# Transposed projection pieces on normed x, in matmuls of 512 columns

## The chip, the cores and the metric

One core of a Trainium2 chip runs one hybrid decoder layer. The metric is the device time of one execution in microseconds, the median of several runs. The engines are TensorE (PE, with its weight loads PEld), VectorE (DVE), ScalarE (ACT), GpSimd (POOL) and SyncE (SP, which here only issues DMAs). Each engine executes its own list of instructions in the order in which the program issues them, and an instruction that waits holds back those behind it on its engine.

## The reference, cut to what matters

The input x has 256 tokens by 1024 channels. The layer normalizes x, multiplies it by one large projection matrix, feeds the columns to four token mixers and a set of gates, merges the branches, and adds an FFN.

```
def rmsnorm(x, w):
    y = xf * lax.rsqrt(jnp.mean(xf * xf, axis=-1, keepdims=True) + NORM_EPS)
    return y * w

h = rmsnorm(x, norm_mix[l])
proj = h @ w_in
(m_z, m_xbc, m_dt, b_qkv, c_qkv, c_f, d_q, d_kv, gate_logits) = jnp.split(proj, SPLIT_POINTS, axis=-1)
y_a = mamba2_branch(m_z, m_xbc, m_dt, ...)     # conv over tokens, SiLU, scan
y_b = moba_attention(bq, bk, bv, ...)
y_c = forgetting_attention(cq, ck, cv, c_f + forget_bias)
y_d = sliding_window_attention(dq, dk, dv, sinks, ...)
gates = sigmoid(gate_logits)
x = x + sum(gates * branch_out) @ w_out
x = x + swiglu(rmsnorm(x, norm_ffn[l]), ...)
```

The factor rsqrt(...) belongs to a token, so it may be multiplied in before the projection or after it.

## The kernel before

**Products in two parts.** Each float32 matrix is split into a hi part (rounded by ACT, `split_hi`) and a lo part (the rest, by DVE, `split_lo`). A product is hi times hi, hi times lo, and lo times hi. The weights come in pieces, named in `FIRST`: `xbc0 n0 qkB0 vB0 vB1 xbc2 qkB1 xbc3 z0 ...`, then gates (`g...`), branch and output projections, `gu` and `dn` of the FFN. A piece is fetched (`fetch`, SP), split in two chunks and multiplied. Three buffers each hold raw, hi and lo weights.

**x of the projection.** `xx(k)` holds channels 128k to 128k+127 of x times `norm_mix`, transposed, as a hi and a lo half of 256 tokens each, side by side. The token factor is not in it. It is multiplied in when a product leaves PSUM: `rb` holds it as a row (times 1, 0.125 and 0.5), `r1` and `r1h` as a column.

**Transposed pieces.** For pieces `qk`, `xbc`, `z` and `qD` the weights (128 columns at a time) are the stationary operand, and the result has channels on partitions. `tr_groups` does two groups for a piece, one for each 128 columns; both fill halves of one PSUM bank. A group is built by `two` and `mm`: for each of 8 k, hi weights times the hi half of x (L264), the same hi weights times the lo half (L265), and after these 8 times lo weights times the hi half (L262): 24 matmuls of 256 columns, each with a weight load of its own. One DVE instruction then takes both halves out of PSUM times `rb`: `end_scaled` (L936) for qk and qD, the first lines of `conv` (L630) and `silu_z` (L661). In natural pieces (`v`, `g`, L1044) x is the stationary operand and weights stream in 512 columns.

**FFN.** Pieces `gu4` and up already work in the other manner: `wide` (L273, L277) multiplies hi weights by both halves of the normalized `x3x` in one matmul of 512 columns, then lo weights by the hi half in 256 columns; `end_ffn` adds the halves of the bank by an ACT copy (L1180) and a DVE addition (L1181).

**The planner.** `Weaver` decides while the program is written where the other engines' work is placed. It holds a clock in nanoseconds for PE, DVE and ACT. `wv.tick(GROUP)` after a group adds 2620 to the PE clock, steps the urgent tasks once, issues chunks of the split (68 + 1.043n on the DVE clock: 1136 for a chunk of 1024) and then steps the other tasks in the order of their list. A task is a generator; each `yield Need(...)` gives the cost of its next step and the buffers that it needs. A step of a task that isn't urgent is refused if it would bring the DVE or ACT clock over the PE clock plus `SLACK` (3500), if the task is ready more than 60 after the clock, or if it has matmuls and is ready over 300 after the PE clock. `wv.until(flags)` asks for none of this: in passes over the list it runs one step of each task for which buffers are free, until the flags are set.

**The tasks at the start.** `conv(0)`, `conv(1)` and `softplus_cums` are started after the first group of qkB0. `softplus_cums` has a DVE reciprocal, then some 27 small POOL instructions (L548 to L564) that end in `av`, then matmuls on `av` (`cum_n`), a DVE copy to `cumn` (L571), two transposes (`cum_t`) and a store. `bias_rows` makes bias rows in `es` and stores them to DRAM. `cb_products` (L674, L675) follows `conv(0)` and `conv(1)`. PSUM has 3 banks tagged acc and 5 tagged att.

Of the kernel before, what the change touches and what calls it, by code (L numbers as in the profile page):

```python
# [25 lines left out]


FIRST = ("xbc0 n0 qkB0 vB0 vB1 xbc2 qkB1 xbc3 z0 qkB2 z1 qkB3 qD0 qkC0 vC0 vC1 qkC1 qD1 qkC2 qkC3").split()

# [177 lines left out]
def hybrid_block_kernel(ctx: ExitStack, tc: tile.TileContext, A, out):  # L207
# [270 lines left out]
        return flat(p)  # L478


    def nat_groups(name, hi, lo, n=256):

        if n == 256:
            p = acc(name, [128, 2, 256])
        else:
            p = [att("%s_%d" % (name, t), [128, n]) for t in range(2)]
        hb, lb = cut(hi, 8, n), cut(lo, 8, n)
        for t in range(2):
            group(p[:, t, :] if n == 256 else p[t],
                  three((lambda k: hb[:, k, :], lambda k: lb[:, k, :]), at_tok(xx, t), range(8)))  # L490
            yield p
# [19 lines left out]
    def bias_rows():  # L511

        yield Need(pe=680, att=1)
        p = att("e", [128, 384])
        for i in range(2):
            pe.matmul(p[32 * i : 32 * i + 8, :], tab[:, 8 * i : 8 * i + 8], oneh[:, i, :], start=True, stop=True)
        yield Need(act=840, w2=2)
        for i in range(2):
            es = work("es%d" % i, [8, 384], "w2")
            act.activation(es, p[32 * i : 32 * i + 8, :], AF.Copy)  # L520
            nc.sync.dma_start(erow[8 * i : 8 * i + 8, :], es)
        rel(att=1, w2=2)
        wv.done.add("erow")

    def softplus_cums():

# [96 lines left out]

    def conv(i, p):

        yield Need(dve=650, w2=2)
        u = work("cu%d" % i, [128, 2, 259], "w2")
        dve.memset(u[:, :, 0:3], 0.0)
        if i > 1:
            dve.tensor_tensor(u[:, :, 3:259], p, rb2(1), ALU.mult)  # L630
            rel(acc=1)
        else:
            for j in range(2):
                dve.tensor_tensor(u[:, j, 3:259], p[j], rb[:, 1, :], ALU.mult)
            rel(**{("att", "acc")[i]: 2})
        c = work("cc%d" % i, [128, 2, 256], "w2")
        th = u[:, :, 0:256]
        for k in range(4):
            if k < 2:
                yield Need(act=620) if k == 0 else Need(dve=800)  # L640
            elif k == 2:
                yield Need(dve=1600)
            for j in range(2):
                g = (2 * i + j + 4) % 8
                if k == 0:
                    act.activation(c[:, j, :], u[:, j, 0:256], AF.Identity, scale=tapsh[:, g, 0:1],
                                   bias=tapsh[:, g, 4:5])
                else:
                    dve.scalar_tensor_tensor(c[:, j, :], u[:, j, k : k + 256], tapsh[:, g, k : k + 1], c[:, j, :],
                                             ALU.mult, ALU.add)  # L650
        act.activation(th, c, AF.Tanh)
        wv.act += 520
        yield Need(dve=1200)
        half_silu(bc[i] if i < 2 else xs[:, 2 * i - 4 : 2 * i - 2, :], c, th)
        rel(w2=2)
        wv.done.add("xbc%d" % i)

    def silu_z(i, p):
        yield Need(dve=600, act=520, w2=2)
        zh = work("zh%d" % i, [128, 2, 256], "w2")  # L660
        dve.tensor_tensor(zh, p, rb2(2), ALU.mult)  # L661
        rel(acc=1)
        th = work("zt%d" % i, [128, 2, 256], "w2")
        act.activation(th, zh, AF.Tanh)
        yield Need(dve=600)
        half_silu(zs[:, 2 * i : 2 * i + 2, :], zh, th)
        rel(w2=2)
        wv.done.add("z%d" % i)

    def cb_products():  # L670
        for g in range(2):
            yield Need(pe=650, att=1)
            p = att("cb%d" % g, [128, 384])
            pe.matmul(p[:, 0:256], bc[0][:, g, 0:128], bc[1][:, g, :], start=True, stop=True)  # L674
# [256 lines left out]
        wv.later(lambda js=js: fox_quad(js), ["qkC%d" % j for j in js] + ["vC0", "vC1", "cum"], True)  # L931


    def end_scaled(name, o, p, r):
        yield Need(dve=600)
        dve.tensor_tensor(o, p, r, ALU.mult)  # L936
        rel(acc=1)
        wv.done.add(name)

    def end_v(br, t, p):  # L940
        yield Need(act=620)
        if br not in v:
            v[br] = slot("v" + br, (128, 2, 512))
        act.activation(v[br][:, t, :], p, AF.Copy, scale=r1[:, t : t + 1])
        rel(acc=1)
        wv.done.add("v%s%d" % (br, t))

    def end_of(name, p):
# [5 lines left out]
        if name[:2] == "qk":  # L954
            br = name[2]
            if i % 2 == 0:
                qk[br, i // 2] = slot(name)
            return end_scaled(name, qk[br, i // 2][:, 2 * (i % 2) : 2 * (i % 2) + 2, :], p, rb[:, 0:2, :])
        if name[:2] == "qD":
            if i == 0:  # L960
                qD.append(slot("qD"))
            return end_scaled(name, qD[0][:, 2 * i : 2 * i + 2, :], p, rb2(0))

    def end_gate(b, nh, t, p):
        yield Need(act=570)
        if nh == 0:
            gates[b, t] = slot("gate%d%d" % (b, t), (128, 1024))
        act.activation(gates[b, t][:, 512 * nh : 512 * nh + 512], p, AF.Tanh, scale=r1h[:, t : t + 1])  # L968
        rel(acc=1)


# [41 lines left out]
            rel(att=1)  # L1013
        wv.done.add("mt%d" % nh)

    rb = const("rb", [128, 3, 256])
    pg = {}
    r1n, r1h = const("r1n", [128, 2]), const("r1h", [128, 2])
    for name in names[1 : names.index("wo00")]:
        if name[:2] == "wb":  # L1020
            b, nh = int(name[2]), int(name[3])
            br = "ABCD"[b]
# [11 lines left out]
        if name[0] in "gv":  # L1034
            b, nh, kh = (int(c) for c in name[1:]) if name[0] == "g" else (name[1], 0, int(name[2]))
            hi, lo = take(name)
            hb, lb = cut(hi, 4, 512), cut(lo, 4, 512)
            for t in (1, 0) if kh else (0, 1):
                if kh == 0:
                    pg[t] = acc("p%s%d" % (name[:-1], t))  # L1040
                terms = three((lambda k: hb[:, k, :], lambda k: lb[:, k, :]),
                              lambda k: xx(4 * kh + k)[:, :, tok(t)], range(4))
# [7 lines left out]
        hi, lo = take(name)  # L1050
        n = sizes[name] // 8
        for p in (nat_groups(name, hi, lo, n) if name[0] == "n" else
                  tr_groups(name, hi, lo, n)):
# [2 lines left out]
        if name == "n0":  # L1056
# [7 lines left out]
            dve.tensor_scalar(r1h, r1, 0.5, None, ALU.mult)  # L1064
# [4 lines left out]
            for i, f in enumerate((1.0, 0.125, 0.5)):  # L1069
                act.activation(rb[:, (1, 0, 2)[i], :], prow, AF.Copy, scale=f)  # L1070
            rel(att=1)
        if name != "n0":
            wv.add(end_of(name, p))
# [305 lines left out]
```

## Time and profile before

| | |
|---|---|
| median of 3 runs | 511.09 us (510.99 to 511.87) |
| the profiled execution, its own time | 511.23 us |
| span, first to last instruction | 509.5 us |
| busy: PE, DVE, ACT, POOL | 501.6, 352.5, 285.6, 30.6 us |
| stretch of the pieces qkB1 to qkC3 | about 48 to 143 us |

The profiled execution's own time lies 1.73 us over its span. Busy time of an engine is the sum of its instructions; the chain of waits is the path from the last instruction back through what released each. In the chain each matmul stands with the time by which it moves the end (its distance from its neighbour), in the timeline with its whole duration, a longer one since matmuls overlap.

### The profile page before, as it was taken

Reading aid. Unit: us, or ns where it says so; the run is one execution under the profiler, and the core shown is the slowest. Engines: PE = TensorE matmul, PEld = TensorE weight load, DVE = VectorE, ACT = ScalarE, POOL = GpSimd, SP = SyncE. Lnnn points to the kernel's source line nnn. Section 1 sums busy time; section 2 is a strip of 40 time slices with the busy share of each in tenths; the row PEclk is TensorE's granted clock in tenths of the full one; section 3 lists DMA queues with packets and bytes.
Section 4 is the critical chain, followed back from the end, with each engine's and each line's share of the span. In section 5 each row is a group of like instructions: output and inputs, shape, how many; then the busy total and the mean of one; then the engine's idle time right before and its main releaser. Section 6 shows DMA issues by size and latency. Waiting matters only on the chain.

```text
span 509.5 us, 7926 instructions
## 1 busy us (share of the span) xinstructions
PE 501.6 (98%) x3106; PEld 443.7 (87%) x3106; DVE 352.5 (69%) x655; ACT 285.6 (56%) x507; POOL 30.6 (6%) x58
## 2 busy tenths in 40 slices
PE   8999999999999999999999999999999999999995
PEld 8988999979988878788888899998888888888884
DVE  5697589697874969496393675688767766764524
ACT  6687356557565747645534435776566655734322
POOL 0008110011220100000000000000000000000000
PEclk9999999999999999999999999999999999999998
DMA  8965545555555464336267291546455445675202
GB/s 307 388 246 185 198 154 214 203 182 180 173 189 184 131 236 152 125 132 282 82 227 268 100 334 67 188 150 237 164 180 219 180 170 204 248 259 222 98 0 82
DMA packets 16161, 96.06 MB, mean 189 GB/s; under 512 B 1979, under 2 KB 2651, under 8 KB 5884
## 3 DMA queue, kind: packets, MB, share of 16 engines
q1 hardware_dynamic: 14844, 91.36, 49.1%
q0 software_dynamic: 1280, 4.20, 2.9%
q8 instruction: 24, 0.39, 0.3%
q14 instruction: 13, 0.11, 0.1%
HBM read 94.46 MB, written 1.09 MB: 188 GB/s over the span
## 4 chain that ended last, share of the span: by engine, by line
PE 96%; DMA 1%; issue 1%; DVE 0%; SPq 0%; ACT 0%; POOLq 0%; POOL 0%
PE pg L1044 17%; PE gu L273 13%; PE pd L1238 11%; PE pb L262 9%; PE gu L277 7%; PE pvC L1044 2%; PE pvB L1044 2%; PE xbc L451 2%; PE qkC L264 2%; PE qkB L262 2%; PE po L262 2%; PE gu L262 2%; PE qkC L265 2%; PE qkC L262 2%; PE qkB L264 2%; PE gu L265 2%
## 5 line engine op out<-in xcount | busy, mean ns | idle before, releaser
L273 PE MATMUL gu<-x3x,hi_gu 128*128 128x512 f32 x288 | 68.7, 391 | 0.0
L1044 PE MATMUL pg<-hi_g,xx 128*128 128x512 f32 x256 | 64.3, 393 | 0.0
L273 PEld LDWEIGHTS gu<-x3x,hi_gu 128*128 128x128 f32 x288 | 52.9, 188 | 10.2
L355 DVE TENSOR_TENSOR lo_gu<-raw_gu,hi_gu 128x1024 fp32r<-128x1024 f32 x44 | 53.3, 1222 | 6.2 <-ACT hi_gu L347 6.2
L1044 PEld LDWEIGHTS pg<-hi_g,xx 128*128 128x128 f32 x256 | 47.4, 188 | 11.0 <-issue 1.5
L1238 PE MATMUL pd<-hi_dn,aa 128*128 128x512 f32 (+1 forms) x176 | 46.6, 387 | 0.0
L347 ACT ACTIVATE hi_g<-raw_g 128x1024 fp32r<-128x1024 f32 x32 | 32.9, 1053 | 23.6 <-DMA raw_g<-in_w_dram 15.7
L347 ACT ACTIVATE hi_gu<-raw_gu 128x1024 fp32r<-128x1024 f32 x44 | 44.0, 1048 | 1.6 <-PE gu L265 1.6
L355 DVE TENSOR_TENSOR lo_dn<-raw_dn,hi_dn 128x1024 fp32r<-128x1024 f32 x22 | 26.1, 1222 | 21.9 <-ACT hi_dn L347 21.8
L355 DVE TENSOR_TENSOR lo_g<-raw_g,hi_g 128x1024 fp32r<-128x1024 f32 x32 | 38.7, 1236 | 2.7 <-ACT hi_g L347 2.7
L1238 PEld LDWEIGHTS pd<-hi_dn,aa 128*128 128x128 f32 x176 | 32.9, 188 | 6.6
L277 PEld LDWEIGHTS gu<-x3x,lo_gu 128*128 128x128 f32 x288 | 36.9, 191 | 1.4
L277 PE MATMUL gu<-x3x,lo_gu 128*128 128x256 f32 x288 | 37.4, 283 | 0.0
L347 ACT ACTIVATE hi_dn<-raw_dn 128x1024 fp32r<-128x1024 f32 x22 | 22.2, 1051 | 25.2 <-PE pd L1238 25.2
L1044 PE MATMUL pg<-lo_g,xx 128*128 128x512 f32 x128 | 34.2, 389 | 0.0
L1181 DVE TENSOR_TENSOR gs<-gu,ge 128x256 f32<-128x256 f32 x36 | 15.2, 424 | 20.1 <-ACT ge L1180 20.1
L1044 PEld LDWEIGHTS pg<-lo_g,xx 128*128 128x128 f32 x128 | 24.0, 188 | 5.0
L1180 ACT ACTIVATE ge<-gu 128x256 f32<-128x256 f32 x36 | 13.8, 384 | 25.5 <-PE gu L277 25.5
L1238 PE MATMUL pd<-lo_dn,aa 128*128 128x512 f32 (+1 forms) x88 | 26.9, 387 | 0.0
L355 DVE TENSOR_TENSOR lo_wb<-raw_wb,hi_wb 128x1024 fp32r<-128x1024 f32 x16 | 19.4, 1221 | 7.4 <-ACT hi_wb L347 7.4
L968 ACT ACTIVATE gate<-pg,r1h 128x512 f32<-128x512 f32 x16 | 11.0, 689 | 20.0 <-PE pg L1044 19.9
L347 ACT ACTIVATE hi_wb<-raw_wb 128x1024 fp32r<-128x1024 f32 x16 | 16.7, 1055 | 7.3 <-PE pg L1044 5.5
(323 smaller groups left out, 1115.9 us busy)
## 6 DMA issues: line engine op xcount, KB each, us to landing
raw_gu<-in_w_dram SPq DMA_DIRECT2D x22, 1024.0 KB, 4.8
raw_g<-in_w_dram SPq DMA_DIRECT2D x16, 1024.0 KB, 4.8
raw_dn<-in_w_dram SPq DMA_DIRECT2D x11, 1024.0 KB, 4.8
raw_wb<-in_w_dram SPq DMA_DIRECT2D x8, 1024.0 KB, 4.9
raw_qkB<-in_w_dram SPq DMA_DIRECT2D x4, 1024.0 KB, 4.9
raw_qkC<-in_w_dram SPq DMA_DIRECT2D x4, 1024.0 KB, 4.8
raw_wo<-in_w_dram SPq DMA_DIRECT2D x4, 1024.0 KB, 4.9
hd<-in_head_dram SPq DMA_DIRECT2D x7, 384.0 KB, 7.4
```

The source lines that it names most:

```text
L262: pe.matmul(o, l, r, start=start, stop=stop)
L264: pe.matmul(o, l, r[:, 0, :], start=start, stop=False)
L265: pe.matmul(o, l, r[:, 1, :], start=False, stop=stop)
L273: pe.matmul(b, wh(k), x(k), start=i == 0, stop=False)
L277: pe.matmul(b[:, 0, :], wl(k), x(k)[:, 0, :], start=False, stop=i == n - 1)
L347: act.activation(parts[name][0][:, s], raws[name][:, s], AF.Copy)
L355: dve.tensor_tensor(lo[:, s], raws[name][:, s], hi[:, s].bitcast(F32), ALU.subtract)
L968: act.activation(gates[b, t][:, 512 * nh : 512 * nh + 512], p, AF.Tanh, scale=r1h[:, t : t + 1])
L1044: pe.matmul(pg[t], l, r, start=kh == 0 and i == 0, stop=kh == 1 and i == len(terms) - 1)
L1180: act.activation(e[:, j, :], p[j][:, 1, :], AF.Copy)
L1181: dve.tensor_tensor(s[:, j, :], p[j][:, 0, :], e[:, j, :], ALU.add)
L1238: pe.matmul(o, l, r, start=start and j == 0, stop=stop and j == len(terms) - 1)
```

## The change

From `qkB1`, the seventh piece, all pieces of the projection use `xr` in place of `xx`: x times `norm_mix` and times the token factor, in a hi and a lo half. `xT` is loaded a second time (`xa`, two DMAs issued on SP when vB0 begins), and eight tasks `normed_x` make the halves. Before qkB1 stands `wv.until` on all eight. The transposed pieces among them (`WIDE`: qkB1, xbc3, z0, qkB2, z1, qkB3, qD0, qkC0, qkC1, qD1, qkC2, qkC3) take a bank of their own for each group and multiply hi weights by both halves in 512 columns. `halves` adds the two halves of a bank. The v and g pieces keep their form, with constant factors at the end in place of columns. `bias_rows` holds its two w2 buffers for two more steps, `cb_products` issues its four matmuls in one step, and the planner's estimate of the POOL work rises from 8600 to 10500.

```diff
+NORMED = FIRST[FIRST.index("qkB1") :]
+WIDE = [n for n in NORMED if n[0] != "v"]
...
+    xa = [slot("xTa%d" % i) for i in range(2)]
+    xr = []
+
+    def normed_x(k):
+        yield Need(dve=400, act=310, w1=1)
+        if not xr:
+            xr.append(parts_of([slot("xr%d" % i, (128, 2, 2, 256), F32R) for i in range(4)]))
+        u = work("xu%d" % k, [128, 256], "w1")
+        dve.scalar_tensor_tensor(u, xa[k // 4][:, k % 4, :], nm_mix[:, k : k + 1], rb[:, 1, :], ALU.mult, ALU.mult)
+        h_, l_ = (xr[0](k)[:, i, :] for i in range(2))
+        act.activation(h_, u, AF.Copy)
+        yield Need(dve=340)
+        dve.tensor_tensor(l_, u, h_.bitcast(F32), ALU.subtract)
+        rel(w1=1)
+        wv.done.add("xr%d" % k)
+
+    def halves(o, p, f=1.0):
+
+        e = work("he", [128, 256], "w1")
+        act.activation(e, p[:, 1, :], AF.Copy, scale=f)
+        if f == 1.0:
+            dve.tensor_tensor(o, p[:, 0, :], e, ALU.add)
+        else:
+            dve.scalar_tensor_tensor(o, p[:, 0, :], f, e, ALU.mult, ALU.add)
+        rel(acc=1, w1=1)
...
-        rel(att=1, w2=2)
+        rel(att=1)
         wv.done.add("erow")
+
+        yield Need(pool=6000)
+        yield Need(dve=1)
+        rel(w2=2)
...
-        yield Need(pool=8600)
+        yield Need(pool=10500)
...
     def cb_products():
-        for g in range(2):
-            yield Need(pe=650, att=1)
-            p = att("cb%d" % g, [128, 384])
+        yield Need(pe=1300, att=2)
+        ps_ = [att("cb%d" % g, [128, 384]) for g in range(2)]
+        for g, p in enumerate(ps_):
             pe.matmul(p[:, 0:256], bc[0][:, g, 0:128], bc[1][:, g, :], start=True, stop=True)
             pe.matmul(p[:, 256:384], bc[0][:, g, 128:256], bc[1][:, g, 128:256], start=True, stop=True)
+        for g, p in enumerate(ps_):
             yield Need(act=420)
...
+    def end_halves(name, o, p, fs):
+        for j in range(2):
+            yield Need(dve=340, act=310, w1=1)
+            while len(p) <= j:
+                yield Need(w1=1)
+            halves(o[:, j, :], p[j], fs[j])
+        wv.done.add(name)
...
-    rb = const("rb", [128, 3, 256])
+    rb = const("rb", [128, 2, 256])
...
     for name in names[1 : names.index("wo00")]:
+        if name == "vB0":
+            for i in range(2):
+                nc.sync.dma_start(xa[i], A["xT"][:, 4 * i : 4 * i + 4, :])
+            for k in range(8):
+                wv.tasks.append(Task(normed_x(k)))
...
+        if name == WIDE[0]:
+            wv.until(["xr%d" % k for k in range(8)])
         hi, lo = take(name)
+        if name in WIDE:
+            hb, lb = cut(hi, 8, 256), cut(lo, 8, 256)
+            p = []
+            for j in range(2):
+                bank = acc(name, [128, 2, 256])
+                for k in range(8):
+                    pe.matmul(bank, hb[:, k, tok(j)], xr[0](k), start=k == 0, stop=False)
+                for k in range(8):
+                    pe.matmul(bank[:, 0, :], lb[:, k, tok(j)], xr[0](k)[:, 0, :], start=False, stop=k == 7)
+                wv.tick(GROUP)
+                p.append(bank)
+                if j == 0:
+                    wv.add(end_of(name, p))
+            continue
```

## Rows read from the trace of the kernel before

**Rows 1.** The page: its span, the busy times, the chain that ended last by engine.

```profile
span 509.5 us, 7926 instructions
PE 501.6 (98%) x3106; PEld 443.7 (87%) x3106; DVE 352.5 (69%) x655; ACT 285.6 (56%) x507; POOL 30.6 (6%) x58
...
PE 96%; DMA 1%; issue 1%; DVE 0%; SPq 0%; ACT 0%; POOLq 0%; POOL 0%
```

**Rows 2.** All waits of PE in the whole span: engine, line, what it waited for, us in total, times, longest.

```profile
PE warm L436 <- DVE cumu L399: 1.1, 1, 1.1
PE xbc L451 <- ACT hi_xbc L446: 0.5, 1, 0.5
```

**Rows 3.** The chain of waits in the FFN, from the last narrow piece to the first wide ones: start, us by which the piece moves the end, what.

```profile
338.72 0.96 PE gu L262 x8
...
341.60 0.96 PE gu L262 x8
342.56 3.65 PE gu L273 x16
...
348.13 3.65 PE gu L273 x16
```

**Rows 4.** Busy time by stretch (start:end, length, then PE, PEld, DVE, ACT, POOL, granted clock, DMA share, GB/s): vB0 and vB1, and xbc2.

```profile
30.20:41.10 10.90, 10.90 (x50) 8.73 (x51) 10.87 (x21) 8.10 (x15) 3.23 (x5) 1.00 0.65 209
41.10:47.95 6.85, 6.85 (x56) 6.21 (x57) 3.41 (x8) 5.27 (x8) 5.57 (x17) 1.00 0.63 233
```

**Rows 5.** The timeline of DVE while PE works on xbc2 and begins qkB1 (start, us, line, operation; in brackets the idle time before it and its releaser).

```profile
39.88 1.22 DVE L355 TENSOR_TENSOR lo_qkB<-raw_qkB,hi_qkB 128x1024 fp32r<-128x1024 f32 x1
41.02 1.66 DVE L649 SCALAR_TENSOR_TENSOR cc<-cu,tapsh,cc 128x256 f32<-128x256 f32 x4
42.61 1.27 DVE L355 TENSOR_TENSOR lo_qkB<-raw_qkB,hi_qkB 128x1024 fp32r<-128x1024 f32 x1
43.80 0.69 DVE L622 SCALAR_TENSOR_TENSOR bc<-cu,cc 128x512 f32<-128x512 f32 x1
...
47.99 0.69 DVE L630 TENSOR_TENSOR cu<-xbc,rb 128x512 f32<-128x512 f32 x1 [3.48 <-PE xbc L262]
48.60 2.40 DVE L355 TENSOR_TENSOR lo_xbc<-raw_xbc,hi_xbc 128x1024 fp32r<-128x1024 f32 x2
```

**Rows 6.** The timeline of POOL in the work that ends in av.

```profile
41.73 0.28 POOL L554 TENSOR_TENSOR sp_p<-sp_p,sp_t 128x32 f32<-128x32 f32 x1
...
48.77 1.15 POOL L559 TENSOR_TENSOR dt<-dt,sp_p 128x32 f32<-128x32 f32 x1
49.90 1.21 POOL L561 TENSOR_SCALAR ea<-ea 128x8 f32<-128x8 f32 x1
...
51.50 0.20 POOL L564 COPY av<-dt 128x16 f32<-128x16 f32 x1
```

**Rows 7.** The chain of waits from the last group of xbc2 on (columns as in rows 3).

```profile
46.99 0.96 PE xbc L262 x8
...
50.84 0.43 PE cb L674 x2
51.27 0.22 PE cb L675 x2
...
54.36 0.58 PE cum_n L262 x6
54.94 0.53 PE cb L674 x2
55.47 0.22 PE cb L675 x2
...
58.55 0.22 PE cum_t L576 x2
```

**Rows 8.** The timelines of DVE and ACT, at places where they run without a pause: a difference in 256 columns and a product of three operands, an ACT copy of 256 columns, and the copy to cumn.

```profile
105.89 0.42 DVE L880 TENSOR_TENSOR yB<-yB,yB 128x256 fp32r<-128x256 f32 x1
106.22 0.48 DVE L720 SCALAR_TENSOR_TENSOR dec<-ac,cumn,smask 128x256 f32<-128x256 f32 x1
...
97.03 0.38 ACT L877 ACTIVATE yB<-yB 128x256 fp32r<-128x256 f32 x1
...
56.93 0.19 DVE L571 COPY cumn<-cum_n 128x32 f32<-128x32 f32 x1
```

**Rows 9.** Busy time us by us behind PE's last matmul (columns as in rows 4; the granted clock is the figure after POOL's busy time).

```profile
503.00:504.00 1.00, 0.30 (x3) 0.16 (x2) 0.62 (x3) 0.26 (x2) 0.00 (x0) 1.00 0.00 0
504.00:505.00 1.00, 0.00 (x0) 0.00 (x0) 0.33 (x3) 0.19 (x1) 0.55 (x1) 0.81 0.00 0
505.00:506.00 1.00, 0.00 (x0) 0.00 (x0) 0.57 (x1) 0.54 (x1) 0.00 (x0) 0.50 0.00 0
```

**Rows 10.** The timeline of PE at the start: the warming matmuls, the first eight of 256 columns, and eight more after a pause.

```profile
1.08 3.78 PE L436 MATMUL warm<-cumu 128*128 128x128 f32 x16 [1.08 <-DVE cumu L399]
4.53 1.99 PE L451 MATMUL xbc<-xx,hi_xbc 128*128 128x256 f32 x8
...
7.48 1.22 PE L451 MATMUL xbc<-xx,hi_xbc 128*128 128x256 f32 x8 [0.49 <-ACT hi_xbc L446]
```

**Rows 11.** The timeline of SP's DMA issues around the place where the two loads of xa are inserted.

```profile
24.47 0.33 SPq L339 DMA_DIRECT2D raw_xbc<-in_w_dram  x1
30.12 0.33 SPq L339 DMA_DIRECT2D raw_qkB<-in_w_dram  x1
```

More of the change, by code (lines that the diff above doesn't have):

```diff
@@ L624, in conv @@
     def conv(i, p):
[L626 to L631, printed above, removed]
-        else:
-            for j in range(2):
-                dve.tensor_tensor(u[:, j, 3:259], p[j], rb[:, 1, :], ALU.mult)
-            rel(**{("att", "acc")[i]: 2})
+        if "xbc%d" % i in WIDE:
+            yield Need(dve=340, act=310, w2=2, w1=1)
+            hold(w2=1)
+            u = work("cu%d" % i, [128, 2, 259], "w2")
+            dve.memset(u[:, :, 0:3], 0.0)
+            for j in range(2):
+                if j:
+                    yield Need(dve=340, act=310, w1=1)
+                while len(p) <= j:
+                    yield Need()
+                halves(u[:, j, 3:259], p[j])
+            rel(w2=1)
+        else:
+            yield Need(dve=650, w2=2)
+            u = work("cu%d" % i, [128, 2, 259], "w2")
+            dve.memset(u[:, :, 0:3], 0.0)
+            if i < 2:
+                for j in range(2):
+                    dve.tensor_tensor(u[:, j, 3:259], p[j], rb[:, 1, :], ALU.mult)
+                rel(**{("att", "acc")[i]: 2})
+            else:
+                dve.tensor_tensor(u[:, :, 3:259], p, rb[:, 1:2, :].broadcast_to([128, 2, 256]), ALU.mult)
+                rel(acc=1)
         c = work("cc%d" % i, [128, 2, 256], "w2")
@@ L658, in silu_z @@
     def silu_z(i, p):
-        yield Need(dve=600, act=520, w2=2)
+        yield Need(dve=340, act=310, w2=2, w1=1)
+        hold(w2=1)
         zh = work("zh%d" % i, [128, 2, 256], "w2")
-        dve.tensor_tensor(zh, p, rb2(2), ALU.mult)
-        rel(acc=1)
+        for j in range(2):
+            if j:
+                yield Need(dve=340, act=310, w1=1)
+            while len(p) <= j:
+                yield Need()
+            halves(zh[:, j, :], p[j], 0.5)
+        rel(w2=1)
+        yield Need(dve=600, act=520, w2=1)
         th = work("zt%d" % i, [128, 2, 256], "w2")
@@ L931, in hybrid_block_kernel @@
         wv.later(lambda js=js: fox_quad(js), ["qkC%d" % j for j in js] + ["vC0", "vC1", "cum"], True)
+    def end_halves(name, o, p, fs):
+        for j in range(2):
+            yield Need(dve=340, act=310, w1=1)
+            while len(p) <= j:
+                yield Need(w1=1)
+            halves(o[:, j, :], p[j], fs[j])
+        wv.done.add(name)
     def end_scaled(name, o, p, r):
@@ L943, in end_v @@
             v[br] = slot("v" + br, (128, 2, 512))
-        act.activation(v[br][:, t, :], p, AF.Copy, scale=r1[:, t : t + 1])
+        act.activation(v[br][:, t, :], p, AF.Copy, scale=r1[:, t : t + 1] if "v%s1" % br not in NORMED else 1.0)
         rel(acc=1)
@@ L957, in end_of @@
                 qk[br, i // 2] = slot(name)
-            return end_scaled(name, qk[br, i // 2][:, 2 * (i % 2) : 2 * (i % 2) + 2, :], p, rb[:, 0:2, :])
+            o = qk[br, i // 2][:, 2 * (i % 2) : 2 * (i % 2) + 2, :]
+            return end_halves(name, o, p, (0.125, 1.0)) if name in WIDE else end_scaled(name, o, p, rb[:, 0:2, :])
         if name[:2] == "qD":
@@ L967, in end_gate @@
             gates[b, t] = slot("gate%d%d" % (b, t), (128, 1024))
-        act.activation(gates[b, t][:, 512 * nh : 512 * nh + 512], p, AF.Tanh, scale=r1h[:, t : t + 1])
+        act.activation(gates[b, t][:, 512 * nh : 512 * nh + 512], p, AF.Tanh, scale=0.5)
         rel(acc=1)
@@ L1037, in hybrid_block_kernel @@
             hb, lb = cut(hi, 4, 512), cut(lo, 4, 512)
+            xs_ = xx if names.index(name) < names.index(WIDE[0]) else xr[0]
             for t in (1, 0) if kh else (0, 1):
@@ L1041, in hybrid_block_kernel @@
                 terms = three((lambda k: hb[:, k, :], lambda k: lb[:, k, :]),
-                              lambda k: xx(4 * kh + k)[:, :, tok(t)], range(4))
+                              lambda k: xs_(4 * kh + k)[:, :, tok(t)], range(4))
                 for i, (l, r) in enumerate(terms):
@@ L1049, in hybrid_block_kernel @@
         first = name == "n0"
+        if name == WIDE[0]:
+            wv.until(["xr%d" % k for k in range(8)])
         hi, lo = take(name)
+        if name in WIDE:
+            hb, lb = cut(hi, 8, 256), cut(lo, 8, 256)
+            p = []
+            for j in range(2):
+                bank = acc(name, [128, 2, 256])
[8 more added lines that the diff above has]
+            continue
         n = sizes[name] // 8
@@ L1068, in hybrid_block_kernel @@
             split_next(1, 2, 2)
-            for i, f in enumerate((1.0, 0.125, 0.5)):
-                act.activation(rb[:, (1, 0, 2)[i], :], prow, AF.Copy, scale=f)
+            for i, f in enumerate((1.0, 0.125)):
+                act.activation(rb[:, 1 - i, :], prow, AF.Copy, scale=f)
             rel(att=1)
```

5 lines of the change are left out of this document (2 added, 3 removed).

## The prediction

> **What bounds the kernel now.** I read the page first. PE is busy 501.6 of 509.5 us and makes 96% of the chain that ended last [rows 1]: what is to be saved lies on PE alone, and work for the other engines is free until it makes PE wait. Then PE's waits: only two, both in the first 8 us [rows 2]. So the cover over everything else holds all along, and each wait that the change brings counts in full. The third view is the chain in the FFN, where the narrow and the wide manner stand side by side. The last views are the stretches and timelines around 38 to 52 us, where the change begins: DVE is full there, 10.87 of 10.90 us, and has slack only in the following 6.85 us, of which it uses 3.41 [rows 4].
>
> **The wide groups.** A narrow group of 24 matmuls takes 341.60 - 338.72 = 2.88 us; a wide piece of two groups takes 348.13 - 342.56 = 5.57, or 2.785 for one [rows 3]. The streamed columns are the same, 6144; what goes is 8 of 24 matmuls with their weight loads, about 12 ns each. 24 groups (12 pieces by 2) save 24 x 0.096 = 2.3 us. The bounds are 2.2 and 2.4 by the rounding of these rows. The order within a piece differs a little from the FFN's (hi and lo groups alternate); I cost that at nothing, since the 24 changes of width could add at most a weight load's fraction of 0.1 us each if not overlapped, up to 2 us, and the natural pieces and the FFN change as often without any wait.
>
> The Trainium skill (TensorE: Matmul & The Clock Gate, Back-to-back issue gap) states a gap of N/2.4 + 2.5 ns for a matmul. By it a narrow group would be 2.62 us and a wide one 2.60, and 24 groups would give 0.5 us where the rows give 2.3. The rows differ from the page here (120 ns for 256 columns, 228 for 512) and I take them.
>
> **Evacuation.** Each group's bank is emptied by an ACT copy and a DVE sum of 256 columns, 0.38 and 0.42 us [rows 8], in place of one DVE instruction of 0.69 for two groups (L630) [rows 5]: 24 x 0.38 = 9.2 us more on ACT, 24 x 0.42 - 12 x 0.69 = 1.8 us more on DVE, over some 95 us. A piece needs two banks where it needed one, so a bank must be empty two groups (5.6 us) after it was filled. The planner lets DVE and ACT be at most 3.5 us ahead of PE's clock, so an urgent step is behind at most that plus 0.8. I cost it at nothing; without that cover one late bank costs a DVE chunk of the split, 1.2 us [rows 5], and I allow up to 5 us for several. Smaller edits (a third ACT row of rb and r1h dropped, constants in place of columns, es held longer) touch instructions with slack: nothing, within 0.2 us either way.
>
> **The preparation.** The two xa loads stand on SP behind the fetch issued at 24.47 and before that of 30.12 [rows 11], which waits for a buffer anyhow, so they are issued by about 25.2 and are there well before their first use at 40; the later fetch isn't delayed. Eight `normed_x` are 8 x (0.40 + 0.35) = 6.0 us on DVE (their spacing when back to back: four L649 in 1.66 [rows 5]; 105.89 to 106.22 [rows 8]) and 3.0 on ACT.
>
> **Where they land** is settled by the planner, and its clock can be followed on paper. After n0 the DVE clock stands at 4678. The ticks add, in order, chunks of 1136 and steps of conv, softplus and qkB0: 7114 after qkB0, +1136 at vB0, 11086 and 13822 after vB0's groups, 16428 after vB1's first. In vB1's second: split 1136, conv(1) 800, so 18364, under a limit of 15720 + 3500 = 19220: two first steps of normed_x fit (400 each). xbc2's first group: limit 22740; 1136 + 1600 + two second steps of 340 reach 22580. Its second: limit 25360; 1136 + 1200 + one first step reach 25316. Without normed_x the same walk gives the order of rows 5 (split, four taps, split, bc), so I trust it. When qkB1 is reached two of the eight are done, one is half done, and `wv.until` issues the rest without any limit, one step of each task in each pass:
> pass 1: DVE cu of conv(2), which needs xbc2's end; PE cum_n; nx2 second; nx3 to nx6 first (then the four w1 buffers are used up); PE cb, all four matmuls.
> pass 2: DVE copy to cumn; nx3 to nx6 second.
> pass 3: two taps of conv(2), PE cum_t, nx7 first.
> pass 4: four taps, nx7 second.
>
> Two PE waits follow. **First**, cum_n now stands before qkB1 on PE and needs av, which POOL finishes at 51.70 [rows 6]; PE is free at 46.99 + 0.96 = 47.95 [rows 7]. Two of POOL's last instructions take 1.15 and 1.21 us where such a one takes 0.28 beside DVE's taps [rows 6]; both ran beside lo_xbc at 48.60 [rows 5], which the new order moves behind the preparation. So av may be there at 51.70 - 0.87 - 0.93 = 49.9 at the earliest, and at 51.7 or, with DVE's new small differences in the way, 52.5. I take 50.4, near the lower end, since the row beside 256-column DVE work is the nearest: a wait of 2.5 us with 0.1 for the hand-over. **Second**, the rest of DVE's list begins with the copy to cumn, after cum_n (0.58), at about 51.1: 0.10 + 4 x 0.35 + 0.80 + 0.40 + 1.6 + 0.42 = 4.7, so xr7 is whole at 55.8. PE does cb (1.40) and cum_t (0.22) meanwhile [rows 7], which are moved, not added, and seven wide matmuls (7 x 0.228), to 54.27: a wait of 1.55. Sum 4.05; with av at the bounds 3.5 to 6.1. Queued behind on DVE is lo_xbc, needed by PE only some 5 us later; on ACT, hi_z. Neither is late.
>
> By the Trainium skill (SBUF - State Buffer, Who interferes with whom) a DVE instruction with two SBUF inputs and a GpSimd one that reads SBUF block each other in full. The taps of conv have two such inputs, and POOL's 0.28 at 41.73 beside them doesn't show it [rows 5, 6]; the split's chunk does. By the rule all of normed_x would block POOL and av would come at 51.7 or later, the time being 1.3 us above mine: the upper half of the range.
>
> **The clock.** The granted clock fell from 1.00 to 0.50 about 1.3 us after PE's last matmul (0.81 in 504 to 505) [rows 9]; a pause of 0.49 us at the start didn't do it. At the start, 6 us after PE's first work, eight matmuls went from 1.99 us to 1.22 [rows 10]. If it falls in the first wait (2.5 us), cum_n, cb, cum_t and seven wide matmuls (3.8 us) take up to twice that, of which the second wait hides 1.55: up to 2.2 us. Between nothing and 2.2 the rows don't decide; I take 0.7.
>
> **Sum against the profiled execution:** 511.23 - 2.3 + 4.05 + 0.7 = 513.7; the median of the runs lies 0.14 below that execution, so 513.5.
>
> **Rivals.**
> A. PE's lists don't meet a wait: the eight are finished in time, or PE has other work before qkB1. Then 511.09 - 2.3 = 508.8. For it: only DVE's order stands in the way, and it has 3.4 us free in xbc2's stretch [rows 4], where the rest of the preparation wants 5 x 0.75 + 0.35 = 4.1; POOL's end would have to come 2.5 us sooner. It decides if the walk above is wrong by 5 x 740 + 340 = 4040 planner units, so that nothing is left for `until` to force. Against it: the walk reproduces rows 5.
> B. The waits come, but shorter: POOL is through at 49.9, DVE's steps close up, the clock holds. 3.5 - 2.3 = +1.2 at least, less some 0.7 if DVE needs no copy behind cum_n: 511.6 to 512.1, hardly told from before.
> C. More waits afterwards: banks or splits late between 60 and 143 us, three or four of 1.2: 517 to 519. For it: DVE is at 99% in some stretches before [rows 4]. Against: PE's delay of 4 us gives the others as much lead.
> D. The wide form doesn't pay, by the page's gap: 0.5 instead of 2.3, that is 515.3.
>
> **Numbers.** The forecast (both waits, 512.2 to 516): 0.56. A 0.22, B 0.10, C 0.08, D 0.04. Range 508.6 to 516.5; of it the likeliest one's own is 512.2 to 516. About 0.2% (1.0 us) is what a measurement here can tell from no change. Faster: A and some 0.01: 0.23. Same: B and a few hundredths of the forecast: 0.13. Slower: 0.64.
>
> **What will show it.** PE's list of waits: cum_n on POOL av (L564) of 2 to 4 us near 48, a matmul of qkB1 on DVE xr of 1 to 2 us near 55. The chain passes through POOL and DVE there. Wide pieces of qkB1 to qkC3 5.57 us apart net of woven work. The granted clock in 50 to 58 us is 1.00 or has a stretch of 0.50. I'm wrong if PE still has only its two early waits, or if its waits lie after 60 us.

## The result, and the profile after

The changed kernel takes 515.55 us in the median of four runs (515.34 to 516.58); the kernel before, run beside it, 511.04 (510.85 to 511.87). The ratio is 1.0082, interval 1.0055 to 1.011. It is slower by 4.5 us in the medians and 4.2 by the ratio, against the 2.4 that were predicted. The profiled execution took 515.34 us.

The page of the changed kernel: span, busy times, and the chain that ended last by engine.

```profile
span 513.6 us, 7594 instructions
...
PE 502.3 (98%) x2914; PEld 434.9 (85%) x2914; DVE 359.5 (70%) x682; ACT 294.5 (57%) x538; POOL 29.6 (6%) x58
...
PE 88%; DVE 5%; POOL 2%; issue 2%; DMA 1%; ACT 1%; SPq 0%; POOLq 0%; ACTq 0%
```

PE has 192 matmuls less and is still busy for longer than before [rows 1]; POOL and more of DVE have come into the chain. All waits of PE in the changed kernel, columns as in [rows 2]:

```profile
PE cum_n L267 <- POOL av L600: 2.9, 1, 2.9
PE warm L441 <- DVE cumu L404: 1.1, 1, 1.1
PE z L1133 <- DVE lo_z L360: 0.7, 1, 0.7
PE ptD L909 <- DVE pD L898: 0.4, 1, 0.4
```

The wait on cumu was there before. The others are new: 4.0 us in three places. The chain of waits of the changed kernel from av on (columns as in [rows 3]), which answers to [rows 7]:

```profile
50.23 0.15 POOL av L600
50.38 0.04 issue
50.42 0.84 PE cum_n L267 x6
51.26 0.94 PE cb L730 x2
52.20 0.43 PE cb L731 x2
52.63 0.85 PE cb L730 x2
53.48 0.43 PE cb L731 x2
53.91 0.43 PE cum_t L612 x2
54.33 2.16 PE qkB L1131 x8
56.49 0.95 PE qkB L1133 x8
57.45 1.84 PE qkB L1131 x8
59.29 0.95 PE qkB L1133 x8
```

The order is the one that was walked on paper: cum_n, all four matmuls of cb and cum_t now stand before qkB1. The last two rows give the wide group: 1.84 + 0.95 = 2.79 us, where a narrow one takes 2.88 [rows 3]. But what stands ahead of them is stretched. cb took 1.40 us and cum_t 0.22 before [rows 7], here 2.65 and 0.43; the first eight wide matmuls took 2.16 in place of 1.84. The busy times us by us in the changed kernel say why (columns as in [rows 4]; the granted clock is the figure after POOL's busy time):

```profile
49.00:50.00 1.00, 0.00 (x0) 0.00 (x0) 1.00 (x3) 0.99 (x3) 0.92 (x4) 1.00 0.22 90
50.00:51.00 1.00, 0.58 (x5) 0.58 (x6) 0.17 (x1) 1.00 (x3) 1.00 (x3) 1.00 0.00 0
51.00:52.00 1.00, 1.00 (x6) 0.82 (x6) 0.70 (x3) 0.60 (x2) 1.00 (x2) 0.62 0.04 12
52.00:53.00 1.00, 1.00 (x5) 0.91 (x4) 1.00 (x4) 0.34 (x1) 0.03 (x1) 0.50 0.80 188
53.00:54.00 1.00, 1.00 (x7) 0.76 (x5) 1.00 (x4) 0.15 (x1) 0.00 (x0) 0.50 0.86 262
54.00:55.00 1.00, 1.00 (x5) 0.85 (x4) 1.00 (x4) 0.80 (x2) 0.00 (x0) 0.67 0.17 61
55.00:56.00 1.00, 1.00 (x7) 0.61 (x5) 0.94 (x3) 0.30 (x1) 0.00 (x0) 1.00 0.00 0
```

PE does nothing from 47.52 to 50.42, then has matmuls again, and the clock falls to 0.50 (1.2 GHz) only after that, for some 3 us. Such a stretch stands in no list of waits: PE counts as busy, its instructions are just longer. The seven pieces from cum_n to the first eight wide matmuls add up to 6.08 us in this chain; at the full clock they are 0.58 + 1.40 + 0.22 [rows 7] + 1.84 = 4.04. So 2.04 us are added there. Whether they are the clock's price is a question for the first experiment.

The timeline of DVE in the changed kernel over the same stretch (columns as in [rows 5]):

```profile
47.56 0.69 DVE L683 TENSOR_TENSOR cu<-xbc,rb 128x512 f32<-128x512 f32 x1 [1.52 <-PE xbc L267]
48.17 0.41 DVE L498 TENSOR_TENSOR xr<-xu,xr 128x256 fp32r<-128x256 f32 x1
48.50 1.67 DVE L494 SCALAR_TENSOR_TENSOR xu<-xTa,chan,rb 128x256 f32<-128x256 f32 x4
51.30 0.19 DVE L607 COPY cumn<-cum_n 128x32 f32<-128x32 f32 x1 [1.14 <-PE cum_n L267]
51.41 1.42 DVE L498 TENSOR_TENSOR xr<-xu,xr 128x256 fp32r<-128x256 f32 x4
52.75 0.88 DVE L698 SCALAR_TENSOR_TENSOR cc<-cu,tapsh,cc 128x256 f32<-128x256 f32 x2
53.54 0.48 DVE L494 SCALAR_TENSOR_TENSOR xu<-xTa,chan,rb 128x256 f32<-128x256 f32 x1
53.94 1.67 DVE L698 SCALAR_TENSOR_TENSOR cc<-cu,tapsh,cc 128x256 f32<-128x256 f32 x4
55.52 0.42 DVE L498 TENSOR_TENSOR xr<-xu,xr 128x256 fp32r<-128x256 f32 x1
```

These are the passes of `wv.until`, in the order predicted. The last `normed_x` is whole at 55.94 (predicted 55.8), and PE's eighth wide matmul, which needs it, comes due just then. The slow clock has used up nearly all the time of the second wait. PE's list of waits has no row for it; only the weight load of that matmul still waits, for 0.27 us:

```profile
55.99 0.19 PEld L1131 LDWEIGHTS qkB<-xr,hi_qkB 128*128 128x128 f32 x1 [0.27 <-DVE xr L498]
```

### The profile page after: what moved, and what is told of

The parts are those of the page before. It is cut to its first block, busy times and chain, and to the rows that moved or that the text cites. A ratio compares the mean times of both kernels' runs of the same rounds, so it can differ in the third digit from the quotient of the medians.

```text
span 513.6 us, 7594 instructions
## 1 busy us (share of the span) xinstructions
PE 502.3 (98%) x2914; PEld 434.9 (85%) x2914; DVE 359.5 (70%) x682; ACT 294.5 (57%) x538; POOL 29.6 (6%) x58
## 4 chain that ended last, share of the span: by engine, by line
PE 88%; DVE 5%; POOL 2%; issue 2%; DMA 1%; ACT 1%; SPq 0%; POOLq 0%; ACTq 0%
PE pg L1116 16%; PE gu L278 13%; PE pd L1325 11%; PE pb L267 8%; PE gu L282 7%; PE qkC L1131 3%; PE pvC L1116 2%; PE xbc L456 2%; PE qD L1131 2%; PE qkB L1131 1%; PE po L267 1%; PE gu L267 1%; PE gu L270 1%; PE po L270 1%; PE gu L269 1%
## 5 line engine op out<-in xcount | busy, mean ns | idle before, releaser
L1116 PE MATMUL pg<-hi_g,xr 128*128 128x512 f32 x256 | 64.2, 393 | 0.0
L1116 PEld LDWEIGHTS pg<-hi_g,xr 128*128 128x128 f32 x256 | 47.5, 188 | 10.7 <-issue 1.2
L1116 PE MATMUL pg<-lo_g,xr 128*128 128x512 f32 x128 | 34.3, 389 | 0.0
L1116 PEld LDWEIGHTS pg<-lo_g,xr 128*128 128x128 f32 x128 | 24.0, 188 | 5.1
L1034 ACT ACTIVATE gate<-pg 128x512 f32<-128x512 f32 x16 | 9.5, 596 | 22.8 <-PE pg L1116 22.8
```

## The experiments

Times are medians; the kernel before was run again beside each batch (511.1 to 511.6 us), so kernels are compared by their ratios to it. Short diffs are against the changed kernel.

**The clock and the second wait.** 22 matmuls whose result nobody uses fill most of the first wait, in an att bank of their own.

```
 def softplus_cums():
...
         yield Need(pe=650, att=1)
+        dm = att("dm", [128, 256])
+        for _ in range(22):
+            pe.matmul(dm, xx(0)[:, 0, 0:128], xx(0)[:, 0, :], start=True, stop=True)
+        rel(att=1)
         p1 = att("cum_n", [128, 2, 16])
```

> 22 matmuls of no use (256 columns, 0.12 us each, 2.64 us) stand before cum_n, where PE waits for POOL. Theory: the granted clock stays 1.00, cum_n, cb and cum_t take 2.2 instead of 4.0 us, but PE then waits for xr7, which DVE has at 55.9 as before, so qkB1's first eight end near 56.2 instead of 56.5: the clock's loss was hidden by the second wait; time 515.2, range 514.7 to 515.6. Rival (the fall of the clock is a cost of its own): 2.0 less, 513.5.

Measured: 515.46 us, ratio 1.0075 (1.005 to 1.01), the span 513.6 as in the changed kernel. The waits of PE that differ near 50 us, a row of the clock, and the end of qkB1's first eight matmuls (a row of the chain of waits), in this run:

```profile
PE qkB L1135 <- DVE xr L498: 1.5, 1, 1.5
...
PE cum_n L267 <- POOL av L600: 0.4, 1, 0.4
```

```profile
52.00:53.00 1.00, 1.00 (x9) 0.91 (x8) 1.00 (x4) 0.49 (x1) 0.12 (x1) 1.00 0.74 180
```

```profile
56.59 0.95 PE qkB L1137 x8
```

With PE at work the clock stays at 1.00, and the second wait stands there at 1.5 us. The first eight matmuls end at 56.59, in the changed kernel at 56.49. cum_n began at 50.52, so the seven pieces take 6.07 us, 2.03 over the full clock, where the changed kernel lost 2.04. Nothing is gained: the wait for xr7 costs these 2 us by itself, and the fall of the clock added nothing to it here. The two lie beside each other, and the longer sets the time. What has to go is the order before qkB1, not the clock's fall.

**The wide form alone.** The same kernel with each wide hi matmul as two of 256 columns.

```
                 for k in range(8):
-                    pe.matmul(bank, hb[:, k, tok(j)], xr[0](k), start=k == 0, stop=False)
+                    for i in range(2):
+                        pe.matmul(bank[:, i, :], hb[:, k, tok(j)], xr[0](k)[:, i, :], start=k == 0 and i == 0, stop=False)
```

> The changed kernel with each hi matmul of 512 columns replaced by two of 256 (same x, same banks, same evacuation, same order of everything else). Theory: the wide form alone saves 24 x 0.09 = 2.2 us in place: 515.55 + 2.2 = 517.7, range 517.0 to 518.3. Rival (by the gap N/2.4 + 2.5 ns the form saves 0.5): 516.0.

Measured: 518.48 us, ratio 1.0129 (1.0103 to 1.0156), just above the expected range; the span is 516.0, that is 2.4 us more. Not all of it is the form, because the clock was at 0.50 for longer in this execution (until 57). Behind that stretch, from the first matmul of z to the first of pg, it took 151.3 - 68.9 = 82.4 us against 148.8 - 67.7 = 81.1. With the wait of z on lo_z at 0.4 in place of 0.7, that is 1.6 us for 20 groups, or 0.08 for each. The gap of N/2.4 + 2.5 ns, which the Trainium skill (TensorE: Matmul & The Clock Gate, Back-to-back issue gap) gives for a matmul by itself, would give 0.02; the trace, in which each matmul has a weight load, doesn't agree with it here.

**Not forcing the other tasks.** Here are three ways to have all eight `normed_x` before the first wide piece without driving softplus, cb and conv: step only those tasks before qkB1 (first diff); put them at the front of the planner's list (second); begin the wide pieces two pieces later (third).

```
-            for k in range(8):
-                wv.tasks.append(Task(normed_x(k)))
+            nx = [Task(normed_x(k)) for k in range(8)]
+            wv.tasks += nx
...
-            wv.until(["xr%d" % k for k in range(8)])
+            while any(t in wv.tasks for t in nx):
+                for t in nx:
+                    if t in wv.tasks and wv.fits(t.need):
+                        wv.run(t)
```

> The loop before qkB1 steps the eight normed_x tasks alone and leaves the other tasks to the planner. Theory (the forced order costs, the wide form saves): no wait of cum_n on POOL, granted clock 1.00 throughout, in their place a wait of 1 to 2 us of qkB1's first matmuls on DVE xr near 48 to 50 us; time 515.55 - 2.9 - 2.0 + 1.2 = 511.8, range 510.5 to 512.5. Rival (two banks per piece and the extra evacuation cost it): still 514.5 or more.

```
-            for k in range(8):
-                wv.tasks.append(Task(normed_x(k)))
+            wv.tasks[0:0] = [Task(normed_x(k)) for k in range(8)]
```

> The eight normed_x tasks stand at the front of the planner's list, ahead of conv(0), conv(1) and softplus_cums, so that all are done before qkB1 and nothing is forced. Theory: no wait of PE on POOL or on xr, clock 1.00; time 515.55 - 2.9 - 2.0 and up to 1 less for the late split near 82 us: 510.6, range 508.8 to 511.2. Rival (banks and evacuation): 514.5 or more. If the loads of xa are late, DVE waits for them near 31 us, 1 to 2 us, without PE waiting.

```
-NORMED = FIRST[FIRST.index("qkB1") :]
+NORMED = FIRST[FIRST.index("z0") :]
```

> The normed x and the wide form begin two pieces later, at z0; qkB1 and xbc3 stay narrow: 20 wide groups instead of 24. Theory: normed_x is done by the planner's own ticks, nothing is forced, no wait near 48 us; 515.55 - 2.9 - 2.0 + 4 x 0.09 = 511.0, range 509.3 to 511.5. Rival (banks and evacuation): 514 or more, since most pieces are unchanged.

Measured: 547.02 (ratio 1.0695, 1.0664 to 1.0725), 541.23 (1.0583, 1.055 to 1.0615) and 541.45 us (1.058, 1.0551 to 1.0609). All three miss, by 30 to 35 us. The wait at cum_n is gone from the list of PE's waits in each. What came instead lies 130 us later. In the run with the tasks at the front, a stretch of busy times (columns as in [rows 4]) and, below it, the matmuls of ya and the first branch projection (duration min/median/max in ns, first and last start in us):

```profile
180.00:210.00 30.00, 15.62 (x94) 10.14 (x94) 22.31 (x89) 15.80 (x51) 1.61 (x3) 0.77 0.10 28
```

```profile
L755 PE MATMUL ya<-dw,xc x16: 379/380/431, 115.1 to 208.0; 128*64 128x256 f32 x16
```

```profile
L267 PE MATMUL pb<-hi_wb,yA x32: 388/393/628, 208.5 to 223.6; 128*128 128x512 f32 x32
```

In the changed kernel ya is done at 126.6 and pb begins at 175.9. Here the second pair of ya comes at 208, right before pb. No projection runs beside it: PE is half idle, DMA at 0.10.

The planner's arithmetic shows how the pair came there. The matmuls of ya belong to two tasks `ssd_quad`, the first and the second pair. The first step of each asks for two of the three `rows` buffers at once, while an attention task asks for one at a time:

```
    BUFS = {... "rows": 3, ...}
...
    def ssd_quad(js):
        yield Need(rows=2)
...
    def att_quad(br, pairs, addend, sinks=None):
...
        for _, _, load_rows, _, _, _ in pairs:
            yield Need(rows=1)
```

The first pair holds two, so one is free. In all three kernels the attention task of qkB2 and qkB3 takes this one before the first pair has given one back. From then on two are never free together when the second pair's turn comes: until the branch projection the planner refuses it every time, and each time for these buffers, never for a clock. This ends only when the first branch projection reaches `wv.until` on yA, which drives all attention tasks in front of the pair, with no projection left to cover them. In the changed kernel, as in the one before, the first pair gives a buffer back first, and the second pair takes both. What made the difference?

**The planner's PE clock.** In the changed kernel the forced pass runs tasks whose ready times lie far ahead, and `run` sets the PE clock to them; on paper the clock is then some 7,300 units further, for 2.2 us of matmuls. Most of it is cum_n's, whose ready time follows from the estimate of 10500 for POOL. The DVE clock moves by about as much, so DVE stays some 3,600 ahead of PE, about `SLACK`, with `normed_x` and much of the other tasks' work done. In the three kernels above that work has to fit under the limit, and later steps come at later groups: the first pair takes its `rows` while qD0 is multiplied, in the changed kernel while z1 is. To test it the clock is set back by 3000 where the wide pieces begin, and nothing else is changed.

```
         hi, lo = take(name)
+        if name == WIDE[0]:
+            wv.pe += -3000
```

> The changed kernel with one line more: the planner's PE clock is set back by 3000 units where the wide pieces begin (all the work and the forced order before qkB1 stay). If that clock, which the forced pass drives ahead, is what keeps the second pair of ya ahead of the branch projections, it must now come after them: the pause of PE between 180 and 210 us appears (some 28 us), the kernel is at 541 to 547 us, while the wait at cum_n stays at 2.9 us. If the pause of the earlier experiments came from other things (from normed_x standing at other places), the time is that of the changed kernel, 515 to 516.

Measured: 542.6 us, ratio 1.0614 (1.0591 to 1.0637). The stretch and ya of this run, and its wait at cum_n:

```profile
180.00:210.00 30.00, 16.10 (x102) 10.14 (x99) 20.76 (x87) 15.83 (x54) 1.62 (x3) 0.77 0.09 28
```

```profile
L755 PE MATMUL ya<-dw,xc x16: 378/380/431, 115.2 to 210.0; 128*64 128x256 f32 x16
```

```profile
PE cum_n L267 <- POOL av L600: 2.9, 1, 2.9
```

The side effect is thus shown: without 3000 units of the forced pass's lead, the same kernel loses 27 us more. In its program the attention task is again ahead of the first pair. The counterparts give that lead to the kernels above by hand: `wv.pe += 1500` with the tasks at the front, `wv.pe += 3000` with only these tasks stepped.

> As the kernel with normed_x at the front of the list, and 1500 added to the planner's PE clock when qkB1 begins, so that its limit on DVE and ACT is looser from there on. On PE the second pair of the scan (ya) then stands before the first branch projection again. Theory (the wide form saves 2.2 us; the forced order at qkB1 costs 5; the 30 us of the three kernels before come from the planner, which in the slower schedule put ya behind the attention chains and so forced all of them at once): no wait of PE over 1 us after the first 10 us, clock 1.00; time 511.04 - 2.2 and up to 1.2 of small late waits: 509.5, range 508.6 to 510.6. Rival (the 30 us come from the preparation itself, DVE and ACT being overloaded): still over 530. Rival (banks and evacuation cost what the wide form saves): 511 or more.

> As the kernel whose loop steps normed_x alone, and 3000 added to the planner's PE clock when qkB1 begins. Theory: the waits of 0.7 and 0.8 us at qkB1 for DVE xr and cu and of 1.2 us for cbs stay, the 20 us of attention waits go; 511.04 - 2.2 + 1.5 to 2.7 = 510.9, range 509.6 to 511.8. Rival (overload by the preparation): over 530.

Measured: 516.86 us (ratio 1.0099, 1.0078 to 1.0119) and 517.52 (1.0103, 1.0063 to 1.0143, its runs 513.96 to 519.26). The pause of 30 us is gone in both, but both miss the expected range, and neither median is below the changed kernel's. In the first, cb stands behind a part of the attention in PE's list; this is the wait that took the place of the other:

```profile
PE cb L730 <- DVE nmB L870: 3.8, 1, 3.8
```

In the second the longest is z on DVE lo_z, 2.5 us, beside 1.5 us in qkB1's first matmuls (0.8 on cu, 0.7 on xr). This is the trace of its fastest run (513.96 us, mean granted clock 0.998); the two above 519 us had 0.989 and 0.986, and what lowered it there is not shown.

**A later start, with the lead.** The whole list may be driven again, but one or two pieces later, when POOL is done: from xbc3 with `wv.pe += 3000`, from z0 with 1500 and with 2250.

> The change with its own wait for all tasks, begun one piece later (at xbc3, 22 wide groups), and 3000 added to the planner's PE clock there. Theory: cum_n is not forced before POOL is done, since one more narrow piece of 5.8 us stands ahead; 511.04 - 2.0 + up to 1.5 = 509.8, range 508.8 to 511. Rival (any forced wait for all tasks costs PE 3 to 5 us, wherever it stands): 513 or more.

Measured: 512.07 us, ratio 1.0005 (0.9992 to 1.0018): above the expected range, and below the rival's 513. So a forced wait for all tasks doesn't cost 3 to 5 us wherever it stands. Among PE's own waits only ptB on pB (0.7) and xbc on xr (0.4) are new. Its weight loads wait for longer, since there a gap shows that a matmul's modelled end covers. Of these, in the run from xbc3:

```profile
PEld xbc L1133 <- DVE xr L498: 0.8, 1, 0.8
...
PEld z L1135 <- DVE lo_z L360: 0.3, 1, 0.3
```

> The wide pieces begin at z0 (20 groups in place of 24), the planner's PE clock is set ahead by 1500 there; nothing else of the changed kernel differs. normed_x has two pieces more to be done in, so no wait is expected near 48 to 56 us and no loss of the clock. Saving of the wide form 20 x 0.092 = 1.8 us. If the waits before qkB1 are the whole of what made the changed kernel slower: 509.2 to 510.2, ratio 0.996 to 0.998. If the rest that was missing in the run that begins at xbc3 (about 1 us) is DVE being short of time between 56 and 82 us (the second half of the evacuation in two steps), part of it stays: 510.2 to 511.2, with a wait of PE or of its weight load on DVE lo_z near 70 to 80 us.

Measured: 537.25 us, ratio 1.0514 (1.0494 to 1.0534): a miss. ya's last matmuls were at 204 us; 1500 was too small a lead.

> The run before, which began the wide pieces at z0 and set the planner's PE clock ahead by 1500, with 2250 in place of 1500. With 1500 the second pair of ya still came behind all of the attention (537 us); with 2250 the order of the instructions has it ahead of the first branch projection again. If that place is what those 26 us hung on, they go whole: the saving of the wide form is 20 x 0.092 = 1.8 us, and the wait of z on DVE lo_z of 1.1 us that the run before had near 70 us stays, since up to there the order is the same: 510 to 511 us, ratio 0.998 to 1.0. If a larger PE clock alone were the reason and not the place of ya, a part only should go: 515 to 530.

Measured: 510.4 us, ratio 0.998 (0.9965 to 0.9995), as expected, and the span 508.7 against 509.5 [rows 1]. Its new wait, and its ya:

```profile
PE z L1135 <- DVE lo_z L360: 1.1, 1, 1.1
```

```profile
L755 PE MATMUL ya<-dw,xc x16: 379/379/430, 109.7 to 127.8; 128*64 128x256 f32 x16
```

This is the only version that beats both kernels, the one before by 0.7 us in the medians and 1.0 by the ratio, just clear of the noise: 20 groups at 0.092 us, less this wait, give 0.7. All 27 us between the last two runs go with the place of ya. In the planner's order the two are nearly the same up to qkC0; there, with 1500, the attention task takes the third of the `rows`, with 2250 the first pair gives one back first.

**The evacuation.** That z keeps waiting for lo_z points to DVE. Rows of the changed kernel's timelines of DVE and of ACT, and a row of its weight loads:

```profile
71.29 0.42 DVE L509 SCALAR_TENSOR_TENSOR zh<-z,he 128x256 f32<-128x256 f32 x1 [1.91 <-ACT he L505]
...
75.39 0.42 DVE L509 SCALAR_TENSOR_TENSOR zh<-z,he 128x256 f32<-128x256 f32 x1 [1.43 <-ACT he L505]
...
80.89 1.22 DVE L360 TENSOR_TENSOR lo_z<-raw_z,hi_z 128x1024 fp32r<-128x1024 f32 x1
```

```profile
70.88 0.39 ACT L505 ACTIVATE he<-z 128x256 f32<-128x256 f32 x1 [0.36 <-PE z L1133]
...
75.00 0.36 ACT L505 ACTIVATE he<-z 128x256 f32<-128x256 f32 x1
```

```profile
82.17 0.53 PEld L1133 LDWEIGHTS z<-xr,lo_z 128*128 128x128 f32 x4 [0.90 <-DVE lo_z L360]
```

DVE stands still before its additions until ACT has copied, twice for a piece, and the split behind is late. The first of these copies (70.88) was not late itself: ACT waited 0.36 us for PE to end the group, and DVE's list has the addition ahead of the split. The second (75.00) followed other ACT work without a pause. In the last run ACT writes the result directly and the addition goes; the product of the hi weights with the lo half of x is then left out.

```
-        act.activation(e, p[:, 1, :], AF.Copy, scale=f)
-        if f == 1.0:
-            dve.tensor_tensor(o, p[:, 0, :], e, ALU.add)
-        else:
-            dve.scalar_tensor_tensor(o, p[:, 0, :], f, e, ALU.mult, ALU.add)
+        act.activation(o, p[:, 0, :], AF.Copy, scale=f)
```

> The changed kernel, but halves() has ACT write the result from the bank's first half at once, and the DVE addition of the second half goes (24 instructions of 0.42 us). This leaves out the product of the hi weights with the lo half of x in the wide pieces. The order of everything else stays. Theory: the waits of PE after 60 us (z on DVE lo_z 0.7, ptD on DVE pD 0.4) and the 0.7 us that had no wait to their name come from the evacuation in two steps: DVE stands still before its additions (1.91 us at 71.3, 1.43 us at 75.4) until ACT's copy is done, and the split behind it is late. Then they go and the time is 1.1 to 1.8 us below the changed kernel's: 513.7 to 514.5, ratio 1.005 to 1.0065, with cum_n's wait still at 2.9 us. Rival: they come from the preparation, which has put DVE's whole list back by some 5 us; then z still waits for lo_z, and the time is 515.1 to 515.6, ratio 1.008 to 1.009.

Measured: 515.21 us (513.94 to 515.86), ratio 1.0064 (1.0041 to 1.0087), whose interval reaches into both expectations. The trace decides more than the time. The waits on lo_z and pD are gone, cum_n's is the same; but in the profiled execution the clock fell sooner, and longer. From its chain of waits:

```profile
50.66 1.46 PE cum_n L267 x6
52.13 1.04 PE cb L726 x2
...
55.30 2.78 PE qkB L1127 x8
```

The seven pieces take 7.42 us in this chain, 1.34 more than in the changed kernel, and it began 0.24 later. qkB1 ends 1.60 us later (61.84 against 60.24), and yet the first FFN piece in the wide manner starts at 346.6 in both. So 1.6 us came back between: without DVE's additions the later waits go. The seven runs say the same. Three have a mean granted clock of 0.993 or 0.994 and take 513.94 to 514.17 us; four, the profiled one among them, have 0.991 and take 515.21 to 515.86. The two fastest runs of the changed kernel have 0.995 and take 515.34 and 515.37. Beside the three runs whose clock is near theirs, that is 1.2 to 1.4 us more, within the theory's 1.1 to 1.8. Whether it is DVE's standing still or just its 10 us of work (24 x 0.42) isn't told apart by this.

## Why the prediction was right or wrong

Right in the direction, in the place and in the mechanism; 2 us too low, and inside the range. Step by step:

- **The wide groups.** 2.79 us for 2.88 in the chain: 24 x 0.09 = 2.2 us were saved (predicted 2.3); 0.08 to 0.09 each by the two ways of measuring. Rival D, the page's gap, is out. The changes of width cost nothing, as assumed, though the reason given for that was partly wrong: the natural pieces are 512 columns wide throughout, and an FFN piece changes half as often.
- **Where they land.** The walk was right on DVE instruction by instruction, including the four passes, and on PE in the moved matmuls. Rival A, no wait, is out: the runs that avoid the order show what it would take, a later start and another planner clock, and then 0.7 to 1.0 us of gain, not 2.3.
- **First wait.** av was there at 50.38 (predicted 50.4), POOL's last instructions were quick again. The wait is 2.9 instead of 2.5 because PE was free 0.43 us sooner in this execution (47.52), in which xbc's wait of 0.5 at the start [rows 2] isn't there; net it is the 2.5 of the prediction. The rule that DVE work with two SBUF inputs contends with GpSimd's reads, by an exclusive lock (Trainium skill: SBUF - State Buffer, Who interferes with whom), would have put av at 51.7 or later; the trace shows a smaller effect at 256 columns. POOL's dt at 48.81 took 0.27 us beside the four products of `normed_x`, where the same instruction beside lo_xbc had taken 1.15 [rows 6]. It wasn't nothing: the two products of av took 0.67 us there, and 0.37 before, where DVE stood still.
- **Second wait and clock.** Predicted 1.55 + 0.7 = 2.25, measured 2.04 together, but otherwise composed. With the clock held at 1.00 by the filling matmuls the second wait alone made 2.03 (1.5 of it in PE's list): it was 0.5 longer than predicted. The fall of the clock then added nothing, the lower of the two bounds, where 0.7 was taken. That the sum of both came within 0.2 of the measurement is luck. In the run without the additions the slow stretch was the longer of the two, and the same pieces lost 3.4.
- **Evacuation at nothing.** This is the term that failed: 1.1 us of named waits (z on lo_z, ptD on pD), and 1.6 us by the run without the additions. The cover that I named (DVE at most 3.5 us ahead of PE's clock) is a limit of the planner's estimates; in DVE's list the additions wait for an ACT copy, which itself waits for PE's group or stands behind other ACT work. Rival C had the mechanism, waits after 60 us, with 1.6 us and not its 3.6 to 4.8.
- **What I didn't see.** That the forced pass also moves the planner's clock, and that 27 us hang on it, by way of three buffers.
- **Slips of arithmetic.** 24 x 0.38 is 9.1 and not 9.2, and Rival B's 3.5 - 2.3 = +1.2 gives up to 512.3 and not 512.1. Neither touches the forecast.

The sum against the two profiled executions (PE's earlier start, the first wait, the second, the evacuation, the wide form): -0.43 + 2.9 + 2.04 + 1.6 - 2.2 = 3.9 us, where the spans differ by 513.6 - 509.5 = 4.1. The last 0.2 have no name.

## What to carry to other kernels

A planner that asks for one thing by forcing everything has two prices, the waits it puts in front of the forced point and the clocks it moves; test each alone before the change behind it is judged. Where a task asks for two buffers at once and others for one, see who is served first: a small shift of the planner's clock can starve it. A wait and the slow clock behind it don't add up: ask which engine is late behind them, and shorten only the longer. When a result takes two engines to leave PSUM, price the standing still of the second in its own list, and look for it in the waits of the weight loads too.

## What was not expected of the hardware

In the changed kernel the granted clock did not fall in the pause of 2.9 us but 0.8 us after PE had begun again, with short matmuls (0.62 in 51 to 52), and was back some 3 us later. Three other runs have a pause of the same 2.9 us before cum_n, and each did it differently. Without the additions the clock was 0.69 in 50 to 51, though PE began only at 50.66: it fell while PE still stood, was back after some 7 us, and the same seven pieces cost 3.4 us over the full clock in place of 2.0. With the wide matmuls halved it fell within 0.4 us of PE's new start, also for some 7 us. With the planner's clock set back it fell nearly 2 us after it, for some 3. So equal pauses have unequal prices from one execution to the next. The mean granted clock of whole runs goes with this: in the run without the additions the seven times lie in two groups at least 1.0 us apart, one at 0.993 to 0.994 and the slower at 0.991. That the length of this one fall makes the two groups is argued, since only one of these runs has a trace.
